# A two-layer DiT on one core: first stage written out for four queues, attention in one written order, modulation units behind block pairs

## The chip, the core and the metric

One NeuronCore of a Trainium2 chip runs the whole program in one launch. Times are device microseconds from the first to the last instruction's work; the figure to move is the median of three runs. The engines are named as in the profile: PE (matmuls; its weight loads are PEld), DVE (elementwise work on vectors), ACT (activation functions and copies), POOL (a second elementwise engine) and SP, whose queue issues most DMAs. Each engine runs its own instructions in order; semaphores hold an instruction until what it reads or overwrites is ready.

## The reference, cut to what matters

A transformer with two layers on 256 image tokens and 256 context tokens (T2 = 512 together), width D = 1024. Each layer is a SwiGLU feed-forward (hidden 2816), a mixer and a second feed-forward. Layer 0 mixes by a short convolution, layer 1 by grouped-query attention (8 heads for queries, 2 for keys and values, head size 128). Before each of them the tokens are normed and modulated by vectors made of the conditioning `c`:

```python
def _rms(t, g):
    y = t32 * lax.rsqrt(jnp.mean(t32 * t32, axis=-1, keepdims=True) + NORM_EPS)
    return y.astype(t.dtype) * g

def _modulate(t, g, shift, scale):
    return _rms(t, g) * (1 + scale) + shift

def _swiglu(h, w13, w2):
    gte, up = jnp.split(h @ w13, 2, axis=-1)
    return (jax.nn.silu(gte) * up) @ w2

def _attend(q, k, v):
    s = jnp.einsum('bqhgd,bkhd->bhgqk', q, k).astype(jnp.float32) * (ATTN_HEAD_DIM ** -0.5)
    p = jax.nn.softmax(s, axis=-1).astype(v.dtype)
    return jnp.einsum('bhgqk,bkhd->bqhgd', p, v)
```

The modulation vectors are `silu(c) @ mod_w + mod_b`, nine of 1024 numbers a layer. All is fp32, and the last feed-forward is needed for the 256 image tokens alone.

## The kernel before, in words

**Layout.** Channels lie on the 128 partitions in KT = 8 tiles, tokens run along the free axis: `x[P, 8, 512]`. S = 256 is one stream (image or context).

**Products.** An fp32 operand is split into a rounded high part and a remainder, and a product is three matmuls, hi·hi, hi·lo and lo·hi (`mm3`, L122 to L124). `split` (L98, L99) makes the parts: ACT copies the high one, DVE subtracts. So each weight tile of 1 MB costs two ACT passes and two DVE passes of 128x1024. Weights come through `load_raw` (L94), which has three raw buffers `wr` of 1 MB; a further load waits until one is free.

**Feed-forward.** The hidden 2816 are 22 tiles, worked in thirds of 8, 7 and 7. Where all 512 tokens take part, tiles are worked in a class `Pair` that saves one of eight block products; its steps are called head, five, six, seven and four, and `seven` of one pair is done between five and six of the next. DVE makes sums of weight and activation blocks for it (`ws`, L557 to L567).

**Modulation vectors.** For layer 0 the first shift and scale (channels 0 and 1) are made by PE: `mod_pe` (L754) multiplies a 1 MB piece of `mod_w` by `sccol` (silu of c), ACT copies the row out, `mod_turn` (L766) turns it onto partitions. Each of four pieces q of each channel serves two channel tiles. The other vectors are made by DVE in 224 units (L142, output tile `junk`), each a multiply-and-sum over 128x1024 read from a `wr` buffer. `tick(n)` adds n to what is owed and issues as many units; `mod_ready` issues what is missing when a vector is needed. Ticks stand in many places, among them two a head in attention and one for each output tile of the projection `wo`.

**First stage.** PE runs WARM = 36 fillers (L726). `square_add` (L220 to L228) squares the eight tiles of x on ACT and sums them on DVE; `rms_inv` sums over partitions (L237), takes root and reciprocal and spreads 1/rms over partitions (L248), once for each stream. Then PE goes by a string of steps, FIRST_STEPS: P is mod_pe, T mod_turn, F the fillers between (FILL = 12), W a weight tile's load and split, N the norm of two channel tiles (`norm_q`: L256 on DVE, L266 and L271 on ACT, L267 on DVE), M the products of weight tile i with quarter q. DVE, ACT and SP are ordered by the scheduler. The first three weight tiles of the feed-forward are worked so, quarter by quarter, 144 matmuls of 128x512 in all. The pieces of `mod_w` use the same three `wr` buffers as the weights.

**Attention.** For each head and each half of 128 queries: `scores` (three matmuls into `psc`; maximum L1042, its negative L1044, exp on ACT L1050 with the sum, reciprocal L1054, product on POOL L1058 into `pn`), `turn` (four transposes L1067 into `pt`, then a split into `pth` and `ptl`), `mix` (twelve matmuls into `pav`, then a split into `a`). All PSUM tiles come from one pool of six banks. `v_proj(2)` and `v_proj(3)` are the last two value projections, among the first scores.

**Projection and last feed-forward.** `wo` gives eight output tiles `py`; each updates x, and gives a raw high and low part of x times the norm's scale, `xa`. The first four weight tiles (L1149 and on in the products `pg` and `pu` from `xa`) use these before 1/rms is known, with a column for the shift; the result is multiplied by 1/rms (`rl`, L1214) behind the product (`first_post`, L1197 to L1200). Meanwhile the normed `h` is made in eight parts: `t` on DVE (L256), high part on ACT (L1226), low part on DVE (L1227). From the fifth tile on the products are from `h` with two matmuls (L1107 for 128x512 and L1108 for 128x256).

Of the kernel before, what the change touches and what calls it, by code (L numbers as in the profile page):

```python
# [16 lines left out]
P = 128  # L17
# [11 lines left out]
WARM = 36  # L29
FILL = 12  # L30
# [4 lines left out]
FIRST_STEPS = (  # L35
    "P10 P00 T10 T00 F W0 N0 W1 M00 W2 M10 P11 M20 P01 T11 T01 N1 M01 P12 M11 P02 T12 T02 N2 "
    "M21 P13 M02 P03 T13 T03 N3 M12 M22 M03 M13 M23 S"
)
# [3 lines left out]
def hybrid_kernel(ctx: ExitStack, tc: tile.TileContext, a: dict, out: bass.AP):  # L42
# [7 lines left out]
    psm = ctx.enter_context(tc.tile_pool(name="psm", bufs=6, space=bass.MemoryType.PSUM))  # L50
    pss = ctx.enter_context(tc.tile_pool(name="pss", bufs=2, space=bass.MemoryType.PSUM))
# [8 lines left out]
    def psum(s="ps"):  # L60
        return psm.tile([P, T2], F32, tag="mm", name=nm(s))

    def psmall(s="pq"):
        return pss.tile([P, T2], F32, tag="sm", name=nm(s))
# [21 lines left out]
    nc.scalar.activation(out=sccol[:, :, :2], in_=ccol, func=AF.Silu)  # L86

# [79 lines left out]
    owed = [0.0]  # L167

    def next_unit():
# [7 lines left out]
        mod_unit(*units.pop(0))  # L177

    def tick(n):

        owed[0] += n
        while (jobs or units) and owed[0] >= 1:
            owed[0] -= 1
            next_unit()
# [348 lines left out]
    class Pair:  # L533
# [66 lines left out]
        def seven(self):  # L600
            self.prod(self.p, "S3", "T3", False)
            nc.vector.tensor_tensor(
                out=self.u[:, S:], in0=self.p, in1=self.gm[:, S:], op=ALU.add
            )
# [6 lines left out]
    def ffn(l, b, h, tot, gate, tail, gs=(), ev=1.5):  # L611
        gs = list(gs)
        i0 = 0
        for t, n in enumerate(THIRDS):
            between = ()
            if tot == T2:
# [22 lines left out]
                for i in range(len(gs), n):  # L639
                    if t == 0 and not heads and i in AS_IS[l, b]:  # L640
# [12 lines left out]
                        if "T1" not in h.t:  # L653
                            h.sums()
                        else:
                            tick(3)
# [9 lines left out]
                    if prev:  # L666
                        prev.seven()
# [53 lines left out]
    idle = psmall("idle")  # L721
# [5 lines left out]

    fill(idle, WARM)
    for k in range(KT):
        square_add(k, 0, T2)  # L730
    ris = []
    for s in range(2):
        ris.append(tp.tile([P, S], F32, name=nm("ris"), tag=f"ris{s}", bufs=1))
        nc.scalar.copy(ris[s], rms_inv(s, (accs[s], accs[s, "last"])))
# [3 lines left out]
    nc.vector.tensor_scalar(  # L738
        out=sb1, in0=modb[:, 0, KT : 2 * KT], scalar1=1.0, scalar2=None, op0=ALU.add
    )  # L740
# [4 lines left out]
    rows = {}  # L745

    def mod_pe(ch, q):


        raw = load_raw(a["mod0"][ch, q])  # L750
        pr = psmall("pr")
        for k in range(KT):
            g = 32 * (k % 4)
            nc.tensor.matmul(  # L754
                pr[g : g + 32, :S], sccol[:, k, :], raw[:, k * S : k * S + S],
# [6 lines left out]
    def mod_turn(ch, q):  # L762
# [13 lines left out]
        )  # L776

    def norm_q(q):
        k2 = slice(2 * q, 2 * q + 2)
        nc.vector.tensor_tensor(  # L780
            out=A00[:, k2, :], in0=A00[:, k2, :], in1=both(normg[:, 0, 0, k2]), op=ALU.mult
        )
        for k in range(2 * q, 2 * q + 2):
            for s in range(2):
                if (q, s) not in h32:
                    h32[q, s] = gp.tile([P, T2], F32, name=nm("hr"), tag="gl" if s else "gh")
                norm_k(s, k, h, A00, B00, ris[s], h32[q, s][:, (k % 2) * S : (k % 2) * S + S])

    pps = [(psum("pg"), psum("pu")) for _ in range(3)]

    ws, gs0 = {}, []

    def load_sc():
# [3 lines left out]

    def first_w(i):
        if i < 2:
            ws[i] = load_w(a["w13"][0, 0, i], fine=True)  # L800
            return
        raw = load_raw(a["w13"][0, 0, i])
        parts = [new_pair("w") for _ in range(4)]
        for j in (0, 2, 1, 3):
            split(*parts[j], raw[:, j * T2 : j * T2 + T2])
        ws[i] = lambda o: tuple(t[:, o % T2 : o % T2 + P] for t in parts[o // T2])

    steps = {
        "P": mod_pe,
        "T": mod_turn,  # L810
        "F": lambda: fill(pps[2][0], FILL),
        "S": load_sc,
        "W": first_w,
        "N": norm_q,
        "M": lambda i, q: w13_mm(pps[i], ws[i], h, range(2 * q, 2 * q + 2), 0, T2),
    }
    with tc.manual_schedule(engines={mybir.EngineType.PE}):
        for step in FIRST_STEPS.split():
            steps[step[0]](*(int(c) for c in step[1:]))
# [6 lines left out]
    convk = cload("convk", [P, 3, KT])  # L826
    qg = cload("qg", [P, 1])
    kg = cload("kg", [P, 1])
    cosT = cload("cosT", [P, S])
    sinT = cload("sinT", [P, S])  # L830
# [74 lines left out]
    pqs = pss.tile([P, T2], F32, tag="sm", name="pqs")  # L905
# [60 lines left out]
    def v_proj(tt):  # L966
        if tt % 2 == 0:
            vt.append(new_pair("v"))
        ps = psum("pv")
# [62 lines left out]

    def scores(hd):
        kv = hd // (HEADS // KVH)
        r_ = []
        for qt in range(2):
            o = (hd % 2) * S + qt * P
            ps = psum("psc")
            mm3(ps, tuple(t[:, o : o + P] for t in qs[hd // 2]), ks[kv], True, True)
            ci = hd * 2 + qt  # L1040
            mx = ap.tile([P, 1], F32, name=nm("mx"), tag="mx", bufs=4)
            nc.vector.reduce_max(mx, ps, axis=AX.X)  # L1042
            nb = ap.tile([P, 1], F32, name=nm("nb"), tag="nb", bufs=4)
            nc.vector.tensor_scalar(  # L1044
                out=nb, in0=mx, scalar1=scq[:, ci : ci + 1], scalar2=-1.0,
                op0=ALU.mult, op1=ALU.mult,
            )
            e = tp.tile([P, T2], F32, name=nm("e"), tag="sg", bufs=3)
            sm = ap.tile([P, 1], F32, name=nm("sm"), tag="smx", bufs=4)
            nc.scalar.activation(  # L1050
                out=e, in_=ps, func=AF.Exp, scale=scq[:, ci : ci + 1], bias=nb, accum_out=sm
            )
            r = ap.tile([P, 1], F32, name=nm("r"), tag="r", bufs=4)
            nc.vector.reciprocal(r, sm)  # L1054
            if qt == 0:
                pn2 = hot("pn", F32)
            pn = pn2[:, qt * T2 : qt * T2 + T2]
            nc.gpsimd.tensor_scalar(out=pn, in0=e, scalar1=r, scalar2=None, op0=ALU.mult)  # L1058
            r_.append(pn)
        return r_  # L1060

    def turn(pn):
        pth, ptl = (hot(t).rearrange("p (b q) -> p b q", q=S) for t in ("pth", "ptl"))
        for qt in range(2):
            pt = psum("pt")
            for kt in range(4):
                nc.tensor.transpose(  # L1067
                    pt[:, kt * P : kt * P + P], pn[qt][:, kt * P : kt * P + P], ident
                )
            split(  # L1070
                pth[:, :, qt * P : qt * P + P], ptl[:, :, qt * P : qt * P + P],
                pt.rearrange("p (k q) -> p k q", k=4),
            )
        return pth, ptl

    aos, at = [], []

    def mix(hd, pt):
# [4 lines left out]
        po = psum("pav")  # L1083
        for kt in range(4):
            vw = tuple(t[:, kv * P : kv * P + P] for t in vs[kt])
            mm3(po[:, :S], vw, (pt[0][:, kt, :], pt[1][:, kt, :]), kt == 0, kt == 3)
        o = (hd % 2) * S
        ah, al = (t[:, o : o + S] for t in at[-1])
        split(ah, al, po[:, :S])
        aos.append((ah, al))  # L1090

    pns, pts = {0: scores(0)}, {}
    v_proj(2)
    v_proj(3)
    pns[1] = scores(1)
    for hd in range(HEADS):
        if hd + 2 < HEADS:
            pns[hd + 2] = scores(hd + 2)
        pts[hd] = turn(pns.pop(hd))
        if hd:  # L1100
            mix(hd - 1, pts.pop(hd - 1))
        tick(2)
    mix(HEADS - 1, pts.pop(HEADS - 1))


# [32 lines left out]
    wo = by_pairs("wo")  # L1138
    for m in range(KT):
        if m == KT - 2:  # L1140
            ready()
        w = wo(m)
        ps = psum("py")
        for k in range(KT):
            mm3(ps[:, :S], w(k), aos[k], k == 0, k == KT - 1)
        gated(m, ps[:, :S], gate)
        square_add(m, 0, S)
# [10 lines left out]
        tick(1)  # L1158
# [46 lines left out]
    ht = []  # L1205
    for i in range(NM):
# [3 lines left out]
        if i < 4:  # L1210
# [6 lines left out]
            if i == 1:  # L1217
                for q in range(4):
                    t = hot("h")
                    ht.append(t)  # L1220
                    for k in (2 * q, 2 * q + 1):
                        o = (k % 2) * T2
                        hi, lo = t[:, o : o + S], t[:, o + S : o + T2]
                        u = scaled(0, k, A, ris)
                        b = B[:, k, :1]
                        nc.scalar.activation(out=hi, in_=u, func=AF.Identity, bias=b)  # L1226
                        nc.vector.scalar_tensor_tensor(  # L1227
                            out=lo, in0=u, scalar=b, in1=hi.bitcast(F32),
# [122 lines left out]
```

## Time and profile before

| | us |
|---|---|
| median of three runs | 1587.46 (1584.85 to 1589.65) |
| the profiled execution, whole | 1589.78 |
| its span in the profile | 1588.0 |
| PE busy in the span | 1565.0 |
| DVE busy | 1319.8 |
| ACT busy | 738.2 |
| POOL busy | 29.8 |

A group of the profile has the line in the kernel, the engine, the operation, output and inputs by the program's names, shapes and count; behind the bar stand busy time, the mean of one in ns and the idle time just before. Matmuls are pipelined: one of 128x512 is shown with some 0.4 us, though the next starts sooner. A row of windows has the busy time of each engine in a stretch and the clock that PE was granted (1.00 is full).

### The profile page before, as it was taken

The page shows a single profiled execution, that of the slowest core. Times are in us where ns is not written, and L with a number is a line of the kernel's source. Part 1 is how long each engine was busy: PE and PEld are TensorE (multiplying, and loading weights), DVE is VectorE, ACT ScalarE, POOL GpSimd, SP SyncE. Part 2 cuts the span into 40 slices and gives each one's busy share as a digit, 9 for nine tenths or more (in the row PEclk, how much of TensorE's full clock was granted, in tenths as well). Part 3 has the DMA queues.
Part 4 walks back from the last instruction along what each step waited for, and adds up shares of the span by engine and source line. Part 5 has one row for each costly group of instructions (what it writes and reads, how often), then busy time and mean ns, then how long its engine had stood idle before and what let it go on. Part 6 is the DMA issues. An engine that isn't in the chain of part 4 may idle for free.

```text
span 1588.0 us, 25040 instructions
## 1 busy us (share of the span) xinstructions
PE 1565.0 (99%) x10210; PEld 1423.9 (90%) x10210; DVE 1319.8 (83%) x2029; ACT 738.2 (46%) x1180; POOL 29.8 (2%) x20
## 2 busy tenths in 40 slices
PE   8999999999999999999999999999999999899998
PEld 6788998998888899989899899899899898888887
DVE  5778778879998879799798899898898899976654
ACT  5532452544322356335345375335255455655543
POOL 0000000000000000000000000000000005200000
PEclk9999999999999999999999999999999999999999
DMA  8545234234565412452342423443433654645552
GB/s 319 181 174 201 92 115 167 104 117 162 186 214 193 177 65 95 142 200 104 130 177 102 160 103 107 158 161 107 175 133 122 235 186 149 234 156 186 186 202 90
DMA packets 38419, 248.74 MB, mean 157 GB/s; under 512 B 5280, under 2 KB 7072, under 8 KB 11936
## 3 DMA queue, kind: packets, MB, share of 16 engines
q1 hardware_dynamic: 35712, 245.38, 43.5%
q10 hardware_dynamic: 2592, 1.76, 0.4%
q8 instruction: 80, 1.31, 0.3%
q14 instruction: 35, 0.29, 0.1%
HBM read 244.77 MB, written 1.05 MB: 155 GB/s over the span
## 4 chain that ended last, share of the span: by engine, by line
PE 93%; DVE 3%; ACT 2%; DMA 1%; issue 1%; POOL 0%; DVEq 0%; POOLq 0%; ACTq 0%
PE py L122 9%; PE py L123 9%; PE py L124 9%; PE p L124 7%; PE p L123 7%; PE p L122 7%; PE q L122 5%; PE q L123 5%; PE q L124 5%; PE py L1107 3%; PE pg L1107 2%; PE pu L1107 2%; PE pg L122 2%; PE pg L123 1%; PE pg L124 1%; PE pu L124 1%
## 5 line engine op out<-in xcount | busy, mean ns | idle before, releaser
L98 ACT ACTIVATE wh<-wr 128x1024 fp32r<-128x1024 f32 (+2 forms) x276 | 277.2, 1015 | 352.2 <-PE py L123 81.2
L99 DVE TENSOR_TENSOR wl<-wr,wh 128x1024 fp32r<-128x1024 f32 (+2 forms) x276 | 319.7, 1166 | 78.4 <-ACT wh L98 71.0
L142 DVE CUSTOM_DVE_ANT_0 junk<-wr,scbc,modb 128x1024 bf16<-128x1024 f32 x224 | 286.8, 1280 | 25.0 <-DMA wr<-in_modT 22.2
L123 PE MATMUL py<-gl,wh 128*128 128x512 f32 (+1 forms) x570 | 213.3, 374 | 0.0
L122 PE MATMUL py<-gh,wh 128*128 128x512 f32 (+1 forms) x570 | 213.3, 374 | 0.0
L124 PE MATMUL py<-gh,wl 128*128 128x512 f32 (+1 forms) x570 | 213.0, 374 | 0.0
L99 DVE TENSOR_TENSOR wl<-ws,wh 128x1024 fp32r<-128x1024 f32 x108 | 131.3, 1223 | 28.6 <-ACT wh L98 28.1
L98 ACT ACTIVATE wh<-ws 128x1024 fp32r<-128x1024 f32 x108 | 113.4, 1058 | 75.1 <-DVE ws L563 32.5
L124 PEld LDWEIGHTS py<-gh,wl 128*128 128x128 f32 x570 | 107.3, 188 | 19.1
L122 PEld LDWEIGHTS py<-gh,wh 128*128 128x128 f32 x570 | 107.4, 188 | 18.5
L123 PEld LDWEIGHTS py<-gl,wh 128*128 128x128 f32 x570 | 107.4, 188 | 18.2
L123 PE MATMUL p<-tl,wh 128*128 128x256 f32 x432 | 122.2, 283 | 0.0
L124 PE MATMUL p<-th,wl 128*128 128x256 f32 x432 | 122.2, 283 | 0.0
L122 PE MATMUL p<-th,wh 128*128 128x256 f32 x432 | 122.2, 283 | 0.0
L122 PE MATMUL q<-bh,wh 128*128 128x256 f32 x320 | 90.6, 283 | 0.0
L123 PE MATMUL q<-bl,wh 128*128 128x256 f32 x320 | 90.6, 283 | 0.0
L124 PE MATMUL q<-bh,wl 128*128 128x256 f32 x320 | 90.6, 283 | 0.0
L122 PEld LDWEIGHTS p<-th,wh 128*128 128x128 f32 x432 | 82.9, 192 | 0.3
L123 PEld LDWEIGHTS p<-tl,wh 128*128 128x128 f32 x432 | 82.9, 192 | 0.3
L124 PEld LDWEIGHTS p<-th,wl 128*128 128x128 f32 x432 | 82.9, 192 | 0.0
L446 DVE SCALAR_TENSOR_TENSOR x<-py,G,x 128x256 f32<-128x256 f32 x144 | 62.9, 477 | 6.3 <-PE py L124 6.0
L557 DVE TENSOR_TENSOR ws<-wr 128x1024 f32<-128x1024 f32 x54 | 65.7, 1218 | 0.0
(296 smaller groups left out, 4181.1 us busy)
## 6 DMA issues: line engine op xcount, KB each, us to landing
wr<-in_w SPq DMA_DIRECT2D x88, 1024.0 KB, 4.9
wr<-in_modT SPq DMA_DIRECT2D x64, 1024.0 KB, 4.8
wr<-in_w2b SPq DMA_DIRECT2D x24, 896.0 KB, 4.6
wr<-in_w2a SPq DMA_DIRECT2D x12, 1024.0 KB, 4.8
wr<-in_mod SPq DMA_DIRECT2D x8, 1024.0 KB, 6.1
wr<-in_cw_cx SPq DMA_DIRECT2D x8, 1024.0 KB, 4.8
wr<-in_w2l SPq DMA_DIRECT2D x8, 1024.0 KB, 4.8
wr<-in_cw_b SPq DMA_DIRECT2D x4, 1024.0 KB, 4.9
```

What stands on the lines that cost most here:

```text
L98: nc.scalar.activation(out=hi, in_=src, func=AF.Copy)
L99: nc.vector.tensor_tensor(out=lo, in0=src, in1=hi.bitcast(F32), op=ALU.subtract)
L122: nc.tensor.matmul(ps, wh, mh, start=first, stop=False, **kw)
L123: nc.tensor.matmul(ps, wh, ml, start=False, stop=False, **kw)
L124: nc.tensor.matmul(ps, wl, mh, start=False, stop=last, **kw)
L142: nc.vector.tensor_tensor_reduce(out=junk, in0=raw[:, j * D : j * D + D], in1=scbc[:, v, :], scale=1.0, scalar=modb[:, l, col : col + 1], ...
L446: nc.vector.scalar_tensor_tensor(out=x[:, m, s * S : s * S + S], in0=ps[:, o : o + S], scalar=g[:, m, s : s + 1], in1=x[:, m, s * S : s * ...
L557: tt(out=sm.rearrange("p (a b c) -> p a b c", a=2, b=2)[:, :, 0, :], in0=a21.unsqueeze(1).to_broadcast([P, 2, T2]), in1=self.raw[:, T2 : 3 ...
L1107: nc.tensor.matmul(ps, w[0], m, start=first, stop=False, skip_group_check=True)
```

## The change

It has four parts.

**1. First stage, written out in order for PE, DVE, ACT and SP.** WARM goes from 36 to 18 and FILL from 12 to 5. The tables for silu and root are loaded by a dummy activation each. Three squares go to DVE, five stay on ACT; squares are added in pairs, and each pair's sum goes into PE's token sums, accumulated over the four pairs. One root, one reciprocal and one spread serve both streams. The pieces of `mod_w` are loaded in halves into tiles of the pool `hop` (16 of them), and no longer into `wr`. The three weight tiles come in two column parts, the first 256 columns of each half, then 768. x/rms is made ahead of the modulation (`over_rms`), and the norm is then one ACT pass with scale and shift for the high part, and two DVE passes. Products alternate between gate and up. Five small constants are loaded by SP instead of ACT. Modulation units are held behind the last norm of this stage.

**2. PSUM pools are made anew for each stage.** `use_banks` closes the pools and opens others; in attention these are two double banks for scores, one double bank for transposes and two banks for the rest.

**3. Attention in one written order for PE, DVE and ACT.** One maximum covers both halves of a head's queries, exp is loaded by a dummy activation before, and `e` is normalised in place by POOL. The output projection's first two tiles start inside the attention. The ticks of attention and of `wo` are gone; each pair's `seven`, when it is done inside the next pair, is followed by `tick(0.5)`.

**4. Last feed-forward.** Five tiles, not four, use the raw `xa`. The normed `h` is made in two halves (`norm_half`), one behind each of tiles 1 and 2: one DVE product of 128x1024, eight ACT passes and two DVE subtractions a half.

```diff
-WARM = 36
-FILL = 12
+FIRST = 5
+WARM = 18
+FILL = 5
...
+        with tc.issue_after(begun[-1].ins):
+            mod_unit(*units.pop(0))
...
                     if prev:
-                        prev.seven()
+                        tick(0.5, prev.seven())
...
+    def over_rms(q, ri):
+        for s in range(2):
+            t = h32[q, s] = gp.tile([P, T2], F32, name=nm("hr"), tag="gl" if s else "gh")
+            nc.vector.tensor_tensor(
+                out=t.rearrange("p (k t) -> p k t", k=2),
+                in0=x[:, 2 * q : 2 * q + 2, s * S : s * S + S],
+                in1=ri[:, s * S : s * S + S].unsqueeze(1).to_broadcast([P, 2, S]), op=ALU.mult,
+            )
...
+    with tc.manual_schedule(engines=set(QUEUES)):
+        for ch, q in ((1, 0), (0, 0)):
+            ask_mod(ch, q)
+        for i in range(3):
+            ask_w(i, 0)
...
+        fill(idle, WARM)
+        for k, eng in enumerate((nc.vector, nc.vector) + (nc.scalar,) * 5 + (nc.vector,)):
+            square(k, eng)
+            if k % 2:
+                pair_sum(k // 2)
+                token_sums(ps, k // 2)
...
+        mod_pe(1, 0)
...
+        over_rms(0, rb)
+        ris = tp.tile([P, T2], F32, name="ris", tag="gm", bufs=3)
+        nc.scalar.copy(ris, rb)
+        mod_pe(0, 0)
+        w_hi(0, 0)
+        w_lo(0, 0)
+        mod_turn(1, 0)
+        mod_turn(0, 0)
...
+        fill(pps[1][0], FILL)
+        norm_q(0)
+        for ch, q in ((1, 1), (0, 1)):
+            ask_mod(ch, q)
+        products(0, 0)
...
+        for i in range(3):
+            ask_w(i, 1)
+        mod_pe(1, 1)
+        mod_pe(0, 1)
...
+    use_banks(("psc", 2), ("ptp", 1), ("pav", 2))
...
+        for hd in range(1, HEADS):
+            turn(hd, 0)
+            if hd + 2 < HEADS:
+                scores(hd + 2)
+            turn(hd, 1)
+            rest(hd, 0)
+            if hd > 1:
+                out_hi(hd - 2)
+                out_lo(hd - 2)
+            rest(hd, 1)
+            if hd + 2 < HEADS:
+                exps(hd + 2)
+            mix(hd - 1)
...
-        tick(1)
...
+            if i in (1, 2):
+                norm_half(i - 1)
```

In the new code `turn` makes the transposes and the ACT copy, `rest` DVE's subtraction, `out_hi` and `out_lo` the split of a head's output, `w_hi` and `w_lo` the split of a weight part, `ask_mod` and `ask_w` the loads.

More of the change, by code (lines that the diff above doesn't have):

```diff
@@ L726, in fill, with table, both @@
             nc.tensor.matmul(ps[:, :P], ones, ones, start=True, stop=True)
[L728 to L734, printed above, removed]
+    def table(f):
+        t = const.tile([P, 1], F32, name=nm("table"), tag="ready")
+        nc.scalar.activation(out=t, in_=eps_t, func=f)
+    def both(t):
+        return t.unsqueeze(2).to_broadcast([P, 2, 2])
     A00 = const.tile([P, KT, 2], F32, name="A00", tag="A00")
@@ new lines, in products @@
+    def products(i, q):
+        if i not in pps:
+            pps[i] = psum("pg"), psum("pu")
+        for k in (2 * q, 2 * q + 1):
+            hh, hl = pick(h, k, 0, T2)
+            w = [w_at(i, (1 - j) * 1024 + k * P) for j in range(2)]
+            for n in range(3):
+                for j in range(2):
+                    nc.tensor.matmul(
+                        pps[i][j], w[j][n == 1], hl if n == 2 else hh,
+                        start=k == 0 and n == 0, stop=k == KT - 1 and n == 2,
+                    )
@@ L796, in load_sc @@
             nc.scalar.activation(out=scbc[:, v, :], in_=scbc[:, v, :], func=AF.Silu)
[L798 to L819, printed above, removed]
+    gs0 = []
     done[0, 0] = done[0, 1] = 16
@@ new lines, in turn, with rest @@
+    def turn(hd, qt):
+        e = es[hd]
+        if qt == 0:
+            pts[hd] = hot("pth"), hot("ptl"), double("ptp", "pt")
+        hi, pt = pts[hd][0], pts[hd][2]
+        for kt in range(4):
+            nc.tensor.transpose(
+                pt[:, qt, kt * P : kt * P + P],
+                e[:, qt * T2 + kt * P : qt * T2 + kt * P + P], ident,
+            )
+        nc.scalar.activation(
+            out=hi[:, qt * T2 : qt * T2 + T2], in_=pt[:, qt, :], func=AF.Copy
+        )
+    def rest(hd, qt):
+        hi, lo, pt = pts[hd]
+        c = slice(qt * T2, qt * T2 + T2)
+        nc.vector.tensor_tensor(
+            out=lo[:, c], in0=pt[:, qt, :], in1=hi[:, c].bitcast(F32), op=ALU.subtract
+        )
@@ L1087, in mix @@
         o = (hd % 2) * S
[L1088 to L1103, printed above, removed]
+        aos.append(tuple(t[:, o : o + S] for t in at[-1]))
@@ new lines, in out_hi, with out_lo, wo_mm @@
+    def out_hi(hd):
+        nc.scalar.activation(out=aos[hd][0], in_=pos[hd][:, :S], func=AF.Copy)
+    def out_lo(hd):
+        nc.vector.tensor_tensor(
+            out=aos[hd][1], in0=pos[hd][:, :S], in1=aos[hd][0].bitcast(F32), op=ALU.subtract
+        )
+    with tc.manual_schedule(engines=set(QUEUES[:3])):
+        scores(0)
+        scores(1)
+        exps(0)
+        exps(1)
+        v_proj(2)
+        scores(2)
+        turn(0, 0)
+        rest(0, 0)
+        exps(2)
+        v_proj(3)
+        turn(0, 1)
+        rest(0, 1)
+        for hd in range(1, HEADS):
[11 more added lines that the diff above has]
+            mix(hd - 1)
+        py2 = double("psc", "py")
+        def wo_mm(m, ks):
+            for k in ks:
+                mm3(py2[:, m, :S], w01[m](k), aos[k], k == 0, k == KT - 1)
+        out_hi(HEADS - 2)
+        out_lo(HEADS - 2)
+        wo_mm(0, range(6))
+        mix(HEADS - 1)
+        out_hi(HEADS - 1)
+        out_lo(HEADS - 1)
+        wo_mm(1, range(6))
+        for m in range(2):
+            wo_mm(m, range(6, KT))
```

339 lines of the change are left out of this document (240 added, 99 removed).

## The prediction

> **What bounds the kernel now.** I read the page first: busy shares, then the chain of work that ended last.
>
> ```profile
> span 1588.0 us, 25040 instructions
> PE 1565.0 (99%) x10210; PEld 1423.9 (90%) x10210; DVE 1319.8 (83%) x2029; ACT 738.2 (46%) x1180; POOL 29.8 (2%) x20
> PE 93%; DVE 3%; ACT 2%; DMA 1%; issue 1%; POOL 0%; DVEq 0%; POOLq 0%; ACTq 0%
> ```
>
> PE carries 93% of the chain, and the change leaves its matmuls nearly as they are. So the time can only move in stretches in which PE isn't streaming. To find those I read busy time by windows (start:end and length; then PE, PEld, DVE, ACT, POOL busy with counts; granted clock; DMA share; GB/s).
>
> ```profile
> 10.00:20.00 10.00, 9.09 (x77) 6.83 (x76) 3.21 (x13) 4.63 (x10) 0.00 (x0) 0.83 0.95 356
> 20.00:30.00 10.00, 9.13 (x48) 6.33 (x50) 9.81 (x19) 9.46 (x20) 0.00 (x0) 1.00 0.75 276
> 30.00:40.00 10.00, 7.95 (x56) 5.17 (x49) 4.71 (x14) 4.04 (x10) 0.00 (x0) 0.90 0.97 385
> 60.00:80.00 20.00, 20.00 (x90) 16.57 (x89) 19.61 (x30) 12.96 (x23) 0.00 (x0) 1.00 0.31 112
> 200.00:240.00 40.00, 40.00 (x324) 39.51 (x323) 31.10 (x40) 21.97 (x34) 0.00 (x0) 1.00 0.35 122
> 1320.00:1340.00 20.00, 17.70 (x107) 15.39 (x106) 18.00 (x48) 11.99 (x26) 13.55 (x7) 0.91 0.36 133
> 1340.00:1370.00 30.00, 24.23 (x173) 21.16 (x172) 29.10 (x64) 16.90 (x40) 16.02 (x10) 1.00 0.42 152
> 1400.00:1420.00 20.00, 16.82 (x126) 16.48 (x126) 15.51 (x33) 11.66 (x26) 0.00 (x0) 0.91 0.36 129
> ```
>
> The middle (60:80, 200:240) is full, so nothing can be gained there, only lost. PE starves in three places: the first stage, attention, and the start of the last FFN. Between 60 and 80 there are 90 matmuls of 128x512 in 20 us; the first began before the stretch and reaches in by up to its 0.39 us, so one takes 20.39/90 = 0.227 us. This is my price of a 128x512 matmul; a 128x256 one is put at half, 0.12.
>
> **First stage.** The time line of before (start, length, engine, line, operation), then groups of 0 to 72 us (busy us, mean ns), then two DMA rows of the page (us to landing).
>
> ```profile
> 9.98 1.28 ACT L220 ACTIVATE sq<-x 128x512 f32<-128x512 f32 x2
> 15.24 3.04 PE L754 MATMUL pr<-wr,sccol 128*32 128x256 f32 x32
> 18.36 0.37 ACT L759 COPY row<-pr 128x256 f32<-128x256 f32 x1 [0.74 <-PE pr L754]
> 19.91 0.51 ACT L266 ACTIVATE hh<-t,mod 128x256 fp32r<-128x256 f32 x1 [1.18 <-DVE mod L771]
> 22.31 0.50 PE L122 MATMUL pg<-hh,wh 128*128 128x512 f32 x1
> 24.48 4.31 SPq L94 DMA_DIRECT2D wr<-in_mod  x2
> ...
> L123 PE MATMUL pg<-hl,wh 128*128 128x512 f32 x25 | 10.3, 414 | 0.1
> L754 PE MATMUL pr<-wr,sccol 128*32 128x256 f32 x128 | 9.5, 426 | 0.0
> L766 PE MATMUL pr<-rowsum,row 128*128 128x2 f32 x32 | 4.8, 256 | 0.0
> L99 DVE TENSOR_TENSOR wl<-wr,wh 128x512 fp32r<-128x512 f32 x12 | 7.4, 689 | 0.0
> ...
> x<-in_xT SPq DMA_DIRECT2D x4, 512.0 KB, 5.0
> wr<-in_mod SPq DMA_DIRECT2D x8, 1024.0 KB, 6.1
> ```
>
> The last x piece is squared at 9.98, but the first product starts at 22.31. Three things lie between: a long row of sums, two modulation products for two vectors, and a late weight split. The next modulation pieces are asked for at 24.48 only, when a weight buffer is free, so PE starves again at 30 to 40 (7.95 busy). From 22.31 to 72 are 49.7 us. In them PE has six groups of 24 to 25 products, 147 x 0.227 = 33.3; three of four modulation rounds, 9.5 - 3.04 = 6.5; and three of four turns, 4.8 x 3/4 = 3.6. So 49.7 - 43.4 = 6.3 us are lost after the first product.
>
> After the change the chain to the first product is: last square and pair sum, 9.98 + 2 x 0.69 = 11.4; token sums, root and reciprocal, 12.8 (four groups for sixteen); modulation 1 beside it; one spread of 1/rms to 15.5; x/rms as two passes of 0.69 on DVE, 16.9; the second vector and its turn, 18.4; split and modulation on DVE to 19.6; hh of two passes to 20.6. So the start moves by -1.7. The mod pieces now have tiles of their own: 2 MB of mod, 0.75 MB of first weight columns and 2 MB of the next mod follow x; at 385 GB/s (30:40) that is 12.3 us, plus small constants now in the same queue, so the next mod lands near 23, where PE finishes its first 12 products (20.6 + 2.7). The later pieces (5.8 us for 2.25 MB, 5.2 for each 2 MB) come ahead of PE's need. The 6.3 lost then go, and the sum is -8.0.
>
> Against that stands the clock. These windows lie on the dips of the granted clock, 3.4 us each:
>
> ```profile
> 10.70:14.10 3.40, 2.51 (x21) 2.37 (x21) 1.50 (x6) 2.37 (x4) 0.00 (x0) 1.00 1.02 403
> 14.10:17.50 3.40, 3.40 (x29) 2.03 (x32) 0.00 (x0) 1.00 (x3) 0.00 (x0) 0.50 0.98 386
> 17.50:20.90 3.40, 3.40 (x39) 2.83 (x32) 1.91 (x7) 1.48 (x5) 0.00 (x0) 0.99 0.87 288
> ```
>
> A stretch in which PE was busy 2.51 of 3.40 us was followed by one at clock 0.50. Before, fillers keep PE busy to 22.2; with 5 for 12, the stretch 17.5 to 20.9 will be thin, and the next, with the first products, at half clock: 3.4/2 = 1.7 lost, with 1.0 taken (0 to 3.4). First stage: -7.0, from -10 (x earlier, no dip) to +0 (mod pieces held by the queue's small loads).
>
> (The Trainium skill, "TensorE: Matmul & The Clock Gate", Part 1: The HAM clock gate, says the clock halves after an idle window of some 3.4 us. The trace agrees in length, but here 2.51 of 3.40 us busy already sufficed. By the page's words a stretch with the turns in it isn't idle, the term would be 0 and the time 1584.0; by the row it is up to 1.7, and 1.0 was taken.)
>
> **Attention.** Groups of 1316 to 1370 us, then the start of the first free-running score matmul and of wo.
>
> ```profile
> L1058 POOL TENSOR_SCALAR pn<-e,r 128x512 f32<-128x512 f32 x16 | 29.6, 1861 | 1331.8 <-DVE r L1054 1328.2 <-DVE bs L99 1.7 <-PE pt L1067 1.4
> L142 DVE CUSTOM_DVE_ANT_0 junk<-wr,scbc,modb 128x1024 bf16<-128x1024 f32 x14 | 17.9, 1275 | 0.0
> L1050 ACT ACTIVATE e<-psc,nb,scq 128x512 f32<-128x512 f32 x16 | 12.4, 777 | 10.1 <-DVE nb L1044 8.5 <-POOL pn L1058 0.9 <-DVE ptl L99 0.8
> L1042 DVE TENSOR_REDUCE mx<-psc 128x1 f32<-128x512 f32 x16 | 10.6, 682 | 0.9 <-PE psc L124 0.9
> L99 DVE TENSOR_TENSOR ptl<-pt,pth 128x512 fp32r<-128x512 f32 x16 | 10.4, 680 | 0.0
> L1067 PE MATMUL pt<-ident,pn 128*128 128x128 f32 x64 | 9.6, 281 | 4.5 <-POOL pn L1058 3.0 <-DVE ptl L99 1.4
> L1044 DVE TENSOR_SCALAR nb<-mx,scq 128x1 f32<-128x1 f32 x16 | 2.8, 204 | 0.0
> ...
> 1319.72 0.40 PE L123 MATMUL psc<-kl,qh 128*128 128x512 f32 x1
> 1367.53 0.39 PE L124 MATMUL py<-a,wl 128*128 128x256 f32 x1 [1.43 <-DVE wl L99]
> ```
>
> From 1319.72 to 1367.53 are 47.8 us. PE's content per head is 6 score matmuls (1.36), 8 transposes (0.9, what 8 take back to back) and 12 mix matmuls (1.44), 3.7 in all; with two value projections of 24 x 0.12 it is 35.4. So 12.4 are lost. DVE is full (18.00 of 20, 29.10 of 30), with 17.9 us of it modulation units, which go. That looks like a gain of up to 12, but the new order closes a loop: there is one double tile for transposes, so the first transposes of a head wait for the last subtraction of the head before. On DVE this stands behind the maximum of the scores, which PE issues after its transposes. The loop is: transposes 0.45 + scores 1.36 + maximum over two banks 1.28 + nb 0.20 + subtraction 0.65 + output's low part 0.4 + subtraction 0.68 = 5.0 against 3.7 of PE work. POOL (two passes a head, 3.7 even at the 1.861 of before) and ACT (two exps, 1.6, and the rest about 1.6) lie beneath. Start-up (scores of two heads, exps, two projections) is 15 by the same rows; then five heads 25.2, one without scores 4.2, and the tail with part of wo 10.4, of which 5.8 is wo's own work: 54.8 - 5.8 = 49.0. So +1 (from -9, the loop not binding, to +4).
>
> **Start of the last FFN.** The wait on PE, then time lines.
>
> ```profile
> PE pg L1107 <- ACT wh L98: 3.2, 1, 3.2
> ...
> 1401.32 0.37 ACT L1214 COPY rl<-ss 128x256 f32<-128x256 f32 x1 [1.00 <-PE ss L248]
> 1406.84 1.28 ACT L1200 ACT_TABLE_LOAD   x1
> 1411.88 1.22 DVE L99 TENSOR_TENSOR wl<-wr,wh 128x1024 fp32r<-128x1024 f32 x1
> L1226 ACT ACTIVATE h<-t,mod 128x256 fp32r<-128x256 f32 x8 | 3.6, 502 | 0.6 <-DVE t L256 0.6
> ```
>
> PE waits 3.2 us for the weights of the fourth tile, which the norm holds up on ACT and DVE; with the half clock behind it the loss is about 5. Now ACT has 16 passes of 0.50 for 8, and the table of Silu besides. Ahead of the fourth tile's split the scheduled order leaves 15 of them, six gate passes and the load: some 11 us from rl to the weights' start, 13 to their low part, against the 8 us of raw tiles that PE has. The stall becomes 5 to 6 and the dip stays: +2.5 (-4, if the fifth raw tile covers it, to +4).
>
> **Pairs.** The ticks of attention and of the output projection (24 units by the code) go behind pairs: half a unit in each of 46, 0.64 us of DVE by the 1.275 of one. In 200:240 DVE has 8.9 of 40 us free, in 60:80 only 0.4. Each unit's raw tile also keeps one of three weight buffers longer. 0 to +12, taken +1. PE's own count grows by a fifth raw tile (48 x 0.12 = 5.8 for 16 x 0.35 = 5.6): +0.2, in the rounding.
>
> **Sum.** -7.0 + 1 + 2.5 + 1 = -2.5: span 1585.5, run 1587.3 (1.8 lie around the span: the profiled run took 1589.8). That run stood 2.3 above the median of three, 1587.46, so 1585.0.
>
> **The rivals.**
> *A, both idle stretches give back most of their loss*: -8 and -9, the others nothing: 1570.5. For it: DVE's 47.1 of 50 us in attention with 17.9 of units. Against: the loop above is longer than PE's work. 0.17.
> *B, slower by the units beside pairs*: PE has no slack there, and where DVE has under 0.64 us free a pair (60:80), a unit of 1.28 us ahead of a subtraction that PE waits for stops it. At 0.45 us for each of 23 units, +10 in place of +1: 1594. For: 19.61 of 20. Against: 31.10 of 40 later. 0.17.
> *C, the first stage does not gain*: its loads now follow one another through one queue with small constants ahead of the second mod piece; a wait of 3 us there, and half clock for two stretches, give -1 in place of -7: 1591. 0.12.
> *D, loop and norm both at their bad end* (+4, +4), first stage as forecast: 1590. 0.1.
>
> **How the numbers follow.** 0.3% of this time, 4.8 us, is about what a measurement can tell from no change. The forecast has 0.44; its own range is 1579 to 1590, and its fast third counts as faster. With A: 0.36 faster. Within 0.3% are the rest of the forecast, C's and D's better parts: 0.38. Slower is B with the worse parts of C and D: 0.26. The range from A's edge to B's is 1573 to 1596.
>
> **What would show it.** First product near 20.6 and the last first-stage product 7 us earlier; a half clock near 20.9 to 24.3; in attention, transposes waiting on DVE's low part in every head, 5.0 us apart, with POOL near 1.6 a pass; a PE wait of 5 us for the weights of the fourth raw tile; no PE idle between 60 and 1270. I am wrong if heads follow at 3.7 to 4.2 us, or if PE loses time in the pairs.

## The result and the profile after

The changed kernel is slower: 1595.66 us (median of four runs, 1595.10 to 1595.99) against 1586.82 for the kernel before; the ratio is 1.0051, 95% interval 1.0038 to 1.0065. By the ratio that is 8.1 us; the span of its profiled execution is 1594.2, 6.2 more than that of before, whose profiled run lay above its median. The forecast was 1585.0, with a range of its own of 1579 to 1590: a little faster or no change.

The page of the changed kernel, then its windows in the stretches that the prediction showed of before, columns as there:

```profile
span 1594.2 us, 24963 instructions
PE 1559.6 (98%) x10192; PEld 1420.5 (89%) x10192; DVE 1317.2 (83%) x1997; ACT 736.3 (46%) x1172; POOL 26.0 (2%) x20
```

```profile
10.00:20.00 10.00, 9.99 (x73) 7.12 (x73) 3.29 (x7) 2.71 (x7) 0.00 (x0) 0.66 1.03 339
20.00:30.00 10.00, 9.24 (x68) 6.22 (x66) 7.03 (x19) 5.63 (x12) 0.00 (x0) 1.00 0.99 348
30.00:40.00 10.00, 10.00 (x60) 7.75 (x59) 8.82 (x21) 5.58 (x11) 0.00 (x0) 1.00 1.03 408
1320.00:1340.00 20.00, 14.92 (x104) 13.06 (x103) 13.99 (x25) 13.29 (x29) 13.30 (x8) 1.00 0.29 103
1340.00:1370.00 30.00, 22.36 (x153) 20.24 (x152) 14.33 (x29) 14.42 (x36) 12.51 (x9) 0.94 0.00 1
1400.00:1420.00 20.00, 13.71 (x102) 13.25 (x101) 14.39 (x24) 16.28 (x33) 0.00 (x0) 0.87 0.19 59
```

At 30 to 40 us PE is now full where it had 7.95 of 10. In attention it is emptier than before (14.92 of 20 and 22.36 of 30, before 17.70 and 24.23), although DVE has fallen from 18.00 to 13.99 and from 29.10 to 14.33: DVE's load went, and PE's wait grew. At the start of the last FFN PE falls from 16.82 to 13.71.

A ledger by stages shows it at once. The marks are start times of matmuls in each trace: the first of the first block pair, the first of the query projection, the last of `wo`, the last of the last FFN's first half, the last of all. Stretches in us, for the kernels of this study too:

| kernel | to first pair | to queries | attention and `wo` | last FFN, first half | its second half |
|---|---|---|---|---|---|
| before | 169.4 | 1100.3 | 120.7 | 131.0 | 62.2 |
| changed | 163.2 | 1103.2 | 125.3 | 135.9 | 62.2 |
| first_only | 163.8 | 1100.4 | 119.4 | 131.0 | 62.2 |
| ticks_only | 164.3 | 1104.1 | 116.1 | 130.2 | 61.0 |
| old_norm | 164.6 | 1105.4 | 125.4 | 130.9 | 62.2 |
| new_norm_4 | 163.0 | 1104.8 | 125.3 | 134.5 | 62.2 |
| old_norm_5 | 163.8 | 1102.6 | 125.5 | 130.9 | 62.2 |
| two_tiles | 164.4 | 1102.4 | 117.6 | 134.8 | 62.2 |
| two_tiles_order | 163.6 | 1102.4 | 118.1 | 134.7 | 62.2 |
| combo | 163.5 | 1102.8 | 117.5 | 129.1 | 61.0 |
| units_low | 163.8 | 1099.0 | 116.8 | 131.0 | 62.2 |
| warm | 167.0 | 1101.6 | 119.3 | 131.0 | 62.2 |
| best | 164.0 | 1103.1 | 116.4 | 129.1 | 61.0 |
| lean | 163.1 | 1100.6 | 117.2 | 129.5 | 62.2 |

For the change: -6.2 + 2.9 + 4.6 + 4.9 + 0 = +6.2, the whole of the span's difference. Three stages lost more than the first gained.

Each row is one execution, and that limits what a single entry tells. In all these traces the granted clock is full or 0.50, and apart from one that the end of the run cuts off a half clock lasts 3.4 us or a multiple of it, so that one such stretch under full PE work costs 1.7 us. One near 570 us, in the middle, shows in ten of the fourteen profiles (not in changed, first_only, combo and units_low), and one between 1328 and 1340 us, in attention, in eight (not in changed, first_only, two_tiles, two_tiles_order, combo and warm). The row of old_norm is its slowest run of twelve (1594.98).

**Attention.** PE's transposes of the changed kernel, with what ended the idle time before each group (start, length, count; idle and releaser in brackets), then DVE in the same stretch:

```profile
1336.26 0.63 PE L1253 MATMUL pt<-ident,e 128*128 128x128 f32 x4 [0.93 <-DVE ptl L1264]
1341.40 0.63 PE L1253 MATMUL pt<-ident,e 128*128 128x128 f32 x4 [1.27 <-DVE ptl L1264]
1346.55 0.63 PE L1253 MATMUL pt<-ident,e 128*128 128x128 f32 x4 [1.27 <-DVE ptl L1264]
1351.70 0.63 PE L1253 MATMUL pt<-ident,e 128*128 128x128 f32 x4 [1.27 <-DVE ptl L1264]
1356.84 0.63 PE L1253 MATMUL pt<-ident,e 128*128 128x128 f32 x4 [1.26 <-DVE ptl L1264]
```

```profile
1343.45 1.23 DVE L1220 TENSOR_REDUCE mx<-psc 128x2 f32<-128x1024 f32 x1 [1.74 <-PE psc L133]
1344.71 0.16 DVE L1222 SCALAR_TENSOR_TENSOR nb<-mx,scq 128x2 f32<-128x2 f32 x1
1344.79 0.68 DVE L1264 TENSOR_TENSOR ptl<-pt,pth 128x512 fp32r<-128x512 f32 x1
1345.39 0.41 DVE L1286 TENSOR_TENSOR a<-po,a 128x256 fp32r<-128x256 f32 x1
1345.72 0.68 DVE L1264 TENSOR_TENSOR ptl<-pt,pth 128x512 fp32r<-128x512 f32 x1
```

Read them together: DVE idles 1.74 us for the scores, then runs maximum, nb, first subtraction, output and second subtraction in one go, to 1346.40; 0.15 later PE may begin the next head, having idled 1.27. A head takes 5.15 us. Then PE waits 1.6 us in sum for two copies of `pth`, in the last two heads, and its last products run at half clock:

```profile
1360.20:1363.60 3.40, 1.61 (x13) 1.33 (x13) 0.97 (x3) 0.81 (x2) 0.21 (x1) 1.00 0.00 0
1363.60:1367.00 3.40, 3.40 (x18) 3.40 (x18) 2.05 (x4) 1.31 (x6) 0.00 (x0) 0.50 0.00 0
```

In the stretch before it PE is busy for only 1.61 of 3.40 us.

**Last FFN.** PE's waits of 1398 to 1460 us, then ACT ahead of the awaited weights:

```profile
PE pg L131 <- ACT wh L107: 6.3, 1, 6.3
PE pg L1335 <- DVE wl L108: 0.7, 1, 0.7
```

```profile
1402.62 0.37 ACT L1470 COPY rl<-ss 128x256 f32<-128x256 f32 x1 [1.00 <-PE ss L263]
1403.01 1.28 ACT L1430 ACT_TABLE_LOAD   x1
...
1412.52 1.08 ACT L1454 ACTIVATE u<-u,mod,A 128x256 f32<-128x256 f32 x2
1413.51 0.40 ACT L107 ACTIVATE g<-gm 128x256 fp32r<-128x256 f32 x1
1413.81 0.59 ACT L1451 ACTIVATE h<-u,mod,A 128x256 fp32r<-128x256 f32 x1
1414.31 1.04 ACT L107 ACTIVATE wh<-wr 128x1024 fp32r<-128x1024 f32 x1
```

From rl to the weights ACT has 11.7 us of work without a gap. PE waits for the fourth tile's weights: 144 products of the first three tiles stand before the wait. The clock behind the wait, of before, then of the changed kernel:

```profile
1413.60:1417.00 3.40, 3.40 (x18) 3.40 (x17) 3.40 (x4) 0.34 (x1) 0.00 (x0) 0.50 0.34 89
1414.80:1418.20 3.40, 1.36 (x6) 1.36 (x6) 2.82 (x3) 3.40 (x5) 0.00 (x0) 0.50 0.00 0
1418.20:1421.60 3.40, 3.40 (x17) 3.20 (x16) 2.42 (x3) 0.48 (x1) 0.00 (x0) 0.50 0.62 202
```

The half clock lasts two stretches in place of one.

### The profile page after: what moved, and what is told of

Its sections match the earlier page's. It is cut to its first block, busy times and chain, and to the rows that moved or that the text cites. A ratio compares the mean times of both kernels' runs of the same rounds, so it can differ in the third digit from the quotient of the medians.

```text
span 1594.2 us, 24963 instructions
## 1 busy us (share of the span) xinstructions
PE 1559.6 (98%) x10192; PEld 1420.5 (89%) x10192; DVE 1317.2 (83%) x1997; ACT 736.3 (46%) x1172; POOL 26.0 (2%) x20
## 4 chain that ended last, share of the span: by engine, by line
issue 81%; PE 12%; DMA 3%; DVE 2%; ACT 1%; POOL 0%; SPq 0%; ACTq 0%; POOLq 0%
PE py L1334 3%; PE pu L1334 2%; PE pg L1334 2%; PE py L1335 1%; DMA mr<-in_mod 1%; PE pg L1335 1%; PE pu L1335 1%; DMA wr<-in_modT 1%; DVE ptl L1264 1%; PE py L131 0%; DMA wr<-in_w 0%; PE py L132 0%; PE py L133 0%; PE pt L1253 0%; DMA normg<-in_normg 0%
## 5 line engine op out<-in xcount | busy, mean ns | idle before, releaser
L107 ACT ACTIVATE wh<-wr 128x1024 fp32r<-128x1024 f32 (+2 forms) x264 | 270.3, 1033 | 343.8 <-PE py L132 111.5
L108 DVE TENSOR_TENSOR wl<-wr,wh 128x1024 fp32r<-128x1024 f32 (+2 forms) x264 | 312.2, 1191 | 66.4 <-ACT wh L107 62.5
```

Of the source, the lines that this page charges most:

```text
L107: nc.scalar.activation(out=hi, in_=src, func=AF.Copy)
L108: nc.vector.tensor_tensor(out=lo, in0=src, in1=hi.bitcast(F32), op=ALU.subtract)
```

## The experiments

Each is measured against runs of the kernel before on the same chip; ratios have their 95% interval. Differences between kernels are taken from the ratios, times 1587; by the two intervals such a difference is good to some 2 to 3 us.

**first_only.** The changed kernel with attention, `wo`, last FFN and ticks of before:

```diff
-                        tick(0.5, prev.seven())
+                        prev.seven()
...
-use_banks(("psc", 2), ("ptp", 1), ("pav", 2))
```

> The changed kernel's first stage and its pools made by stage, with attention, projection, last FFN and all ticks of the kernel before. If the first stage alone gives the 6.2 us by which the first pair starts earlier, and the 2 us lost again between 100 and 1300 us belong to the half units behind the pairs: about 6 below the kernel before, near 1581, and PE loses in 62 to 1310 us what it lost before. Rival, the loss in that stretch belongs to the pools made by stage or to the shifted first stage itself: near 1583, with the loss of the changed kernel in the same places.

1583.03 us, ratio 0.9971 (0.9962 to 0.9980): 4.6 below the kernel before. The ledger has it: first pair 5.6 earlier, the middle 1100.4 as before. So the first stage carries its gain to the end, and neither the new pools nor it is seen to cost the middle anything.

**old_norm, new_norm_4, old_norm_5.** The last FFN, taken apart: norm and tile count as before; new norm with four raw tiles (FIRST = 4); old norm with five.

> The changed kernel with the norm of the last FFN and the four raw tiles as before. If the 16 passes of the new norm on ACT hold up the weights of the fourth tile (PE waited 6.3 us for them, before 3.2), this stretch takes 131 us again in place of 136: 4.5 to 5 below the changed kernel, near 1591. Rival, the stall comes from what reaches the last FFN from ahead (weights loaded late, buffers held, the projection's banks): no change, 1595.

> The changed kernel with four raw tiles and its new norm. If the 16 ACT passes stall the weights of the fourth raw tile, the wait of 6 us stays: within 1 of the changed kernel, 1595. Rival, the fifth raw tile is the cost: 4 to 5 below it.

> The changed kernel with the norm of before and five raw tiles. If the ACT passes are the cost, 4 to 6 below the changed kernel, as old_norm. Rival, the fifth raw tile is the cost: within 1 of the changed kernel.

old_norm 1590.99, ratio 1.0018 (1.0007 to 1.0029), 5.2 below the changed kernel; old_norm_5 1591.43, ratio 1.0021 (1.0013 to 1.0029), 4.8 below; new_norm_4 1595.71, ratio 1.0048 (1.0036 to 1.0060), the same as the changed kernel. PE's wait for weights is 3.2 us in the two with the old norm, 6.3 in new_norm_4. It is not the same wait: with the old norm, as in the kernel before, ACT makes the high parts of the fourth tile between passes of the norm, and PE stops four products later, at a product of the fifth tile; with the new norm it stops at the fourth. The norm is the cost, and the fifth raw tile is worth nothing that these runs can tell.

**two_tiles and two_tiles_order.** Two single banks for the transposes, and in the second DVE's first subtraction ahead of the maximum:

```diff
-    use_banks(("psc", 2), ("ptp", 1), ("pav", 2))
+    use_banks(("psc", 2), ("ptp", 2), ("pav", 2))
...
-            pts[hd] = hot("pth"), hot("ptl"), double("ptp", "pt")
+            pts[hd] = hot("pth"), hot("ptl"), []
...
+        pt = banks["ptp"].tile([P, T2], F32, tag="t", name=nm("pt"))
...
             turn(hd, 0)
+            rest(hd, 0)
             if hd + 2 < HEADS:
                 scores(hd + 2)
             turn(hd, 1)
-            rest(hd, 0)
```

> The changed kernel with two single banks for the transposes in place of one double bank, so that the first transposes of a head wait only for the first subtraction of the head before. If the loop through the one tile sets the 5.15 us a head, a head takes 4.1 to 4.3 us (the first subtraction still stands behind the maximum), 4 to 5 below the changed kernel, near 1591. Rival, the chain of maximum, exps and POOL's product sets it: 5.15 stays, 1595.

> As two_tiles, and DVE's first subtraction of a head is written ahead of the maximum of the scores. If the loop is through DVE's order and the tile, nothing is left to wait for but PE's own 3.65 us a head: 3.7 to 4.0 us a head, 6 to 8 below the changed kernel, near 1588.5. Rival, the chain of maximum, exps and POOL: 4.5 us or more, no better than two_tiles.

two_tiles: 1588.13, ratio 1.0004 (0.9995 to 1.0014), 7.5 below the changed kernel. two_tiles_order: 1588.04, ratio 0.9998 (0.9988 to 1.0009), no different from it. A head takes 4.4 us in both. Transposes of two_tiles, then of two_tiles_order:

```profile
1339.05 0.63 PE L1255 MATMUL pt<-ident,e 128*128 128x128 f32 x4 [0.44 <-DVE ptl L1266]
1343.44 0.63 PE L1255 MATMUL pt<-ident,e 128*128 128x128 f32 x4 [0.52 <-DVE ptl L1266]
```

```profile
1337.50 0.66 PE L1255 MATMUL pt<-ident,e 128*128 128x128 f32 x4 [0.73 <-POOL e L1243]
1341.90 0.66 PE L1255 MATMUL pt<-ident,e 128*128 128x128 f32 x4 [0.50 <-POOL e L1243]
1346.30 0.66 PE L1255 MATMUL pt<-ident,e 128*128 128x128 f32 x4 [0.50 <-POOL e L1243]
```

The single tile did set the pace. The ledger's attention is 7.7 us shorter, and up to 1.7 of that is the half clock at the end of attention: the profiles of all four kernels with the double tile have it, those of the three with two tiles don't. The second expectation, 3.7 to 4.0 us a head, missed: with DVE's wait gone, PE waits for POOL's normalising, at the end of scores, maximum, exps and reciprocal. POOL itself idles 1.29 us a head there. DVE and ACT of two_tiles_order in one head show what sets 4.4:

```profile
1340.98 1.21 DVE L1220 TENSOR_REDUCE mx<-psc 128x2 f32<-128x1024 f32 x1
1342.62 0.78 ACT L1234 ACTIVATE e<-psc,nb,scq 128x512 f32<-128x512 f32 x1 [1.52 <-DVE nb L1222]
1344.15 1.08 ACT L1259 ACTIVATE pth<-pt 128x512 fp32r<-128x512 f32 x2
1344.77 0.69 DVE L1266 TENSOR_TENSOR ptl<-pt,pth 128x512 fp32r<-128x512 f32 x1 [0.26 <-ACT pth L1259]
1345.38 1.21 DVE L1220 TENSOR_REDUCE mx<-psc 128x2 f32<-128x1024 f32 x1
```

The subtraction now ahead of the maximum waits for ACT's copy, the copy stands behind the exps, and the exps wait for the maximum one turn earlier: from maximum to maximum 4.40 us, with hardly a gap on the way. So the new order took one loop apart and closed another of the same length. This is read from the trace; no run changes that order again.

**combo.** two_tiles and old_norm together.

> two_tiles and old_norm together. If the two stalls are apart from each other, their gains add: 7.5 and 5.2 below the changed kernel, near 1583. Rival, one hides part of the other: 1586 or more.

1583.16, ratio 0.9963 (0.9951 to 0.9975): 14.0 below the changed kernel, for 7.5 and 5.2 apart. The two gains add, so the stalls are separate.

**ticks_only.** On first_only, the units alone are moved; attention's order stays that of before:

```diff
-                        prev.seven()
+                        tick(0.5, prev.seven())
...
-        tick(2)
     mix(HEADS - 1, pts.pop(HEADS - 1))
...
-        tick(1)
```

> first_only with the half units behind the pairs, and without the ticks of attention and projection, which are else as before: the move of the units by itself. If these units cost the stretch from the first pair to the queries 2 to 5 us (1103 to 1105 us in the three kernels that have them, 1100 in the two that don't), this stretch is 2 to 5 longer than in first_only. If DVE, 94% busy, bounds the attention of before, its 120 us from queries to the end of the projection become 4 to 8 shorter; then 1 to 4 below first_only in all. Rival, the attention of before is bound by the chain of scores, maximum, exps and POOL, not by DVE's load: 0 to 2 shorter, and 1 to 3 above first_only.

1582.35, ratio 0.9964 (0.9951 to 0.9978), 1.1 below first_only, which the intervals don't tell from nothing. Attention takes 116.1 us for 119.4, 3.3 less, although this profile has a half clock there and that of first_only has none; so DVE's load costs the attention of before some 3 to 5 us, not the 8 to 12 that its fullness suggests: without units PE still waits there, for POOL and then for DVE. The middle takes 3.7 more, of which up to 1.7 is the half clock near 570 us, which first_only's profile doesn't have either. PE's waits that the profiles list between the first pair and the queries are 5.9 us for 3.1. The longest, of ticks_only, then of first_only:

```profile
PE py L132 <- DVE gl L108: 1.5, 1, 1.5
PE pv L133 <- DVE wl L108: 1.3, 2, 0.8
PE pq L131 <- ACT hh L281: 0.9, 1, 0.9
```

```profile
PE q L133 <- DVE wl L108: 0.8, 1, 0.8
PE pg L131 <- ACT wh L107: 0.7, 1, 0.7
PE ss L252 <- ACT sq L235: 0.5, 1, 0.5
```

The first of them has its cause on DVE, in ticks_only:

```profile
885.10 0.68 DVE L623 TENSOR_TENSOR gm<-sg,p 128x512 f32<-128x512 f32 x1
887.65 1.28 DVE L151 CUSTOM_DVE_ANT_0 junk<-wr,scbc,modb 128x1024 bf16<-128x1024 f32 x1 [1.87 <-DMA wr<-in_modT]
888.86 0.08 DVE L151 DVE_READ_ACCUMULATOR2_ANT mod<- 128x1 f32 x1
888.86 0.68 DVE L108 TENSOR_TENSOR gl<-gm,gh 128x512 fp32r<-128x512 f32 x1
```

DVE waits 1.87 us for a unit's 1 MB of data, with the subtraction that PE needs queued behind the unit. Here it is not that DVE is full, but that a unit whose data has not landed stops what stands behind it.

**units_low.** first_only with one tick a head, none in `wo` or behind pairs:

```diff
-        tick(2)
+        tick(1)
     mix(HEADS - 1, pts.pop(HEADS - 1))
...
-        tick(1)
```

> first_only with one tick a head in attention in place of two and none in the projection, so that no unit stands behind pairs and the last eight fall into the last FFN. If units in attention cost time there (119.4 us from queries to the end of the projection with them, 116.1 without) and units behind pairs cost it in the middle (1104 against 1100 us), this is below both: the middle near 1100.4, attention near 117.5, 1 to 2 below first_only. Rival, what is forced at the projection stops DVE there: no gain over first_only.

1579.14, ratio 0.9944 (0.9930 to 0.9958): 8.9 below the kernel before, 4.3 below first_only. Attention takes 116.8 us, the middle 1099.0. The gain is larger than expected. Of the 4.0 us between the two profiles 1.4 lie in the middle, where the code is that of first_only; no run shows that the edit makes them.

**warm, best, lean.** Fillers in the first stage, on first_only (warm) and on units_low (best, lean):

```diff
-WARM = 18
+WARM = 30
...
                 token_sums(ps, k // 2)
+                fill(idle, (3, 3, 6, 0)[k // 2])
```

In lean there are 25 fillers ahead and none between.

> first_only with 30 fillers ahead and 3, 3 and 6 of them between the token sums, so that PE isn't thin before the first modulation products. If the half clock from 11 to 18 us costs what its rows show (products 1.93 and spread 2.08 us in place of about 1.0 each), the clock is full there, the first product starts some 2 us sooner, and the run is 1.5 to 2 below first_only. Rival, what PE then waits for is the landing of the next mod piece: below 0.5.

> units_low and warm together. If both theories hold, 3 to 4 below first_only, near 1579 where the kernel before has 1588.

> units_low with 25 fillers ahead and none between the sums, so that PE passes from fillers to token sums with little gap and the sums aren't held up. If the half clock from 10 to 17 us is what is left to gain, the sums end near 12.4 us in place of 13.4, the first product comes 1.5 to 2.5 sooner and the run is about 2 below units_low, 0.993 of the kernel before. Rival, as in warm: the fillers hold up the sums, or the next mod piece sets the pace; no gain, 0.994 to 0.995.

warm 1584.96, ratio 0.9980 (0.9967 to 0.9992); best 1581.45, ratio 0.9961 (0.9949 to 0.9973); lean 1578.46, ratio 0.9941 (0.9928 to 0.9953). The first two missed: they are 1.4 above first_only and 2.7 above units_low. Modulation product and spread of first_only, then of warm:

```profile
13.57 1.93 PE L826 MATMUL pr<-mr,sccol 128*32 128x256 f32 x16
15.43 2.08 PE L922 MATMUL rb<-ident,rs 128*128 128x128 f32 x8
```

```profile
16.18 1.07 PE L826 MATMUL pr<-mr,sccol 128*32 128x256 f32 x16
17.18 1.16 PE L923 MATMUL rb<-ident,rs 128*128 128x128 f32 x8
```

The clock is full there, and each row is 0.9 shorter, as expected. But fillers stand in PE's queue ahead of the token sums: the product that follows the sums starts at 16.18 in place of 13.57, and the first product of the FFN at 23.24 for 22.41. In this profile the half clock then comes at 22.5 to 29.3 us, on the first products (granted 0.50 over 24 to 27), and the first pair is 3.2 later. In best it doesn't come: the clock is full up to 570 us, and yet its first product is at 22.57 and its first pair at 164.0, where units_low has 22.24 and 163.8. So what the clock gave back, the fillers took. Why best is 2.7 above units_low isn't shown: in its profile the middle is 4.1 longer, where the two have the same code. lean takes the fillers between the sums away: its first product is at 21.33, 0.9 before units_low. Yet the run is only 0.5 below units_low, inside both intervals: a half clock now lies on 20 to 24 us (granted 0.61), on the first products.

## Why the prediction was wrong

By its own steps:

- *First stage, -7.0.* Near: -6.2 in the profile, and first_only holds -4.6 (0.9971) to the end. The parts were off. The first product came at 21.77, not 20.6: 0.5 earlier than before, where 1.7 stood. The half clock lay earlier than the step said, on 11.9 to 18.7 us and not on 20.9 to 24.3, with the modulation products and the spread, whose rows take 1.93 and 2.08 us where warm has 1.07 and 1.16 at full clock. Behind the first product 5.7 were gained, for 6.3 less 1.0 of clock.
- *Attention, +1.* The loop was read rightly: 5.15 us a head for 5.0, and 25.4 for five heads where 25.2 stood (1331.44 to 1356.84), with POOL at 1.63 a pass. Start-up was 15.5 for 15. The step that failed is the tail: from the last head's transposes at 1361.32 to the end of `wo` at 1391.7, less its 23.0 of products, are 7.4 us, where the step had 10.4 - 5.8 = 4.6. The half clock at 1363.6 to 1367.0, 1.7 us, and a wait of 1.0 in `wo` for DVE's update of x make up 2.7 of these 2.8; the step had neither. Measured +4.6, above the upper bound of +4.
- *Start of the last FFN, +2.5.* Right in mechanism, by old_norm and new_norm_4; mis-sized, +4.9. The stall is 6.3 where 5 to 6 was forecast, 3.1 more than before. A second wait of 0.7 for the next weights was not in the sum. Of the clock the step said only that the dip stays; it lies on 1.4 and 3.4 us of PE's work where before had 3.4, 0.7 more lost. With the 0.2 of the fifth raw tile, 4.7 of the 4.9 are named. The upper bound, +4, was too near. The lower one, a fifth raw tile that covers the stall, has no ground: the stall is in the fourth, and with four raw tiles it is the same (new_norm_4). The reading of before was off too: its 3.2 us end with the fifth tile's high part (line L1107, 1412.85), while the fourth's low part, the row at 1411.88, was ready at 1413.10.
- *Pairs, +1.* Measured +2.9; six profiles without units behind pairs have 1099.0 to 1103.1 in the middle, eight with them 1102.4 to 1105.4, in the mean 2.6 more. The two groups overlap, and a single pair of profiles tells little. The step counted 23 more units in the middle; the traces have 184 `junk` units there for 174, and eight more in the last FFN. It looked for DVE's free time in the pairs. PE in fact waits at the stages' ends and in the convolution, one case being a unit that waited for its data ahead of `gl`: between 62 and 1310 us its listed waits are 6.3 for the 2.3 of before.
- *Rival A* fell in the new order, as the forecast said, and mostly also in the old one: with no units its attention gave 3 to 5 us, not 9. *Rival B* has the nearest time, 1594, by a path that didn't happen: its price of the units was +10, and they cost 2.9. *Rival C* fell with first_only. *Rival D* is the nearest in what happened: both stretches past their bad ends. In the chances, 0.17 and a third of 0.44 make 0.32 for faster, not 0.36; the time doesn't hang on it.

So no single mechanism failed: three losses were each priced low, by 3.6, 2.4 and 1.9 us, and together they are 7.9 of the 8.7 us between the forecast span, 1585.5, and the measured one; the first stage is the rest. What the sum lacked was the price of the tails. Behind a stretch in which PE was busy 1.61 of 3.40 us (attention) or not at all (1411.4 to 1414.8, last FFN) its next products ran at half clock; and in `wo` and the last FFN PE waited 1.0 and 0.7 us for work of DVE that the sum didn't have.

POOL's product shows the units' side of the matter. In ticks_only, without units beside it, it is

```profile
L1227 POOL TENSOR_SCALAR pn<-e,r 128x512 f32<-128x512 f32 x16 | 25.8, 1622 | 1331.3 <-DVE nb L1213 1322.5 <-PE pav L133 5.5 <-PE pt L1236 3.4
```

1622 ns a pass where before had 1861 and first_only 1927. The Trainium skill, "SBUF — State Buffer", section "SBUF: two separate sides", says that a DVE operation with two SBUF inputs and a POOL operation that reads SBUF lock each other out; a unit is such an operation, and the means agree in direction. No run here shows a single pass blocked for a whole unit.

Against the changed kernel, the old order of attention without units takes 116.1 us, the new order 125.3, and the new order with two tiles 117.5. So the double tile in the written order is 7.7 of the 9.2 us between the two (125.3 to 117.6 in two_tiles); taking the units out helped.

## What to carry to other kernels

Where an order is written by hand, follow each buffer round its loop: one double tile turned a stage with half of DVE's time free into one that waits for DVE in every head, and splitting the tile gave 7.5 us. Moving one operation to break a loop can close another: follow the new one round as well. Spare work put into a queue costs by what stands behind it when its data is late, so give it a place where its data has landed. units_low, the first stage of the change with half of the units taken out of attention, beats both kernels: 0.9944 of the kernel before (0.9930 to 0.9958).

## What the runs showed that I had not expected

In the last FFN a 128x512 matmul that alternates with a 128x256 one goes start to start in 0.236 to 0.237 us in eleven profiles and in 0.230 in three (ticks_only, combo, best), with the 128x256 one at 0.117 in all, and the granted clock at full. Over its two halves that is some 3 us: combo has 190.1 in the ledger, old_norm, with the same code there, 193.1. In ticks_only it is 2.0 us against first_only (191.2 for 193.2), more than the 1.1 by which that run is shorter. It may be a part of the spread of single runs (1584.85 to 1589.65 for the kernel before); what sets it was not tried.
